# An S5 and mLSTM layer on one core: an early load moved to another buffer, a banked output projection, and eight weight scales computed earlier

## Chip, core and metric

The kernel runs on one core of a Trainium2 chip. The metric is the device time of one execution in microseconds (us). TensorE (PE) multiplies matrices into PSUM banks; VectorE (DVE) and ScalarE (ACT) read those banks; GpSimd (POOL) works on SBUF; all transfers are issued by SyncE (SP) on one queue, in order.

## What is computed

One layer on a sequence of 2048 positions with 1024 features: a norm, a projection that feeds two mixers side by side (an S5 state-space scan with a GLU, and four mLSTM heads), an output projection with residual, and a feed-forward network (FFN) with residual. Cut from the reference:

```
h = rmsnorm(x, norm_mix_g[l])
p = h @ w_in[l]
u, q_raw, k_raw, v, o_raw, i_raw, f_raw = jnp.split(p, cuts, axis=-1)
y_ssm = s5_mixer(u, ...)
y_ml = mlstm_mixer(q_raw, k_raw, v, o_raw, i_raw, f_raw, ...)
x = x + jnp.concatenate([y_ssm, y_ml], axis=-1) @ w_out[l]
h = rmsnorm(x, norm_ffn_g[l])
x = x + jnp.square(jax.nn.relu(h @ w_ff1[l])) @ w_ff2[l]
return rmsnorm(x, final_norm_g)
```

## The kernel before

Every product of large matrices is made from three matmuls of 16-bit halves (hi*hi, hi*lo, lo*hi), so every weight block is loaded as 32-bit numbers into a staging buffer, its largest absolute value is found, a power of two is derived from it as scale, and the block is split into two 16-bit halves.

For the weights of the projections, load_w does this: it loads into `st`, a tile of the pool stg, which has one buffer, so a load waits until the block before it has been split. w_scale (L107 to L122) reduces the tile on VectorE (mx, m), spreads the maximum over all partitions with one matmul against the identity (pmx, all_max, L98), reduces that (ma, L100) and derives the scale sg. L140, L141 and, for the u block, L134 to L137 split. The names end in vo0, qk0 and u0 for the first blocks that are used.

At the start the sequence is read in 16 tiles xt0 to xt15 of 128 positions (norm_x: L438 to L441 norm them into xs, L446 transposes xs on TensorE into pt, L448 and L449 split pt into xn). Products of the first half with vo0 (pv), qk0 (pq) and u0 (pu) follow. The S5 tiles uz0 and uz1, in the pool big, receive pu.

After sixteen mLSTM blocks and the S5 units the output projection runs: out_proj(t, m) makes one 128x512 tile, for a quarter t of the sequence and a tile m of eight features, from 24 matmuls into a PSUM tile po (mm3, L159 to L161). VectorE then adds it to x (L1053, the only reader of po, which so frees its bank), and squares are summed for the next norm (L1027, L1028). t=0 is mixed with the GLU of the S5 branch, t=1 runs alone, t=2 and t=3 alternate together with hprep, which prepares the seven operands of the FFN (one level of Strassen-Winograd; L1087 to L1123). The column sums ss_f and the rows rb_f are the FFN's norm. w_out comes in four blocks st_out0 to st_out3 through load_w; the residual tiles come as x2_0 to x2_3 (accx) and, for t of 2 and 3, tile by tile.

The FFN runs over 16 units of w1 (a0 to a15) and of w2 (b0 to b15), in two phases. In phase 0 every unit's scale is made when it has been loaded: f_scale (L1201 reduces 128x2048 to one column, pmx_a or pmx_b spreads it, six small operations follow), called by w1_scale and w2_scale. w_split (L1231, L1232) splits. fx, fv and fw are the products with w1, read into e and split into hid; gx, gv and gw those with w2, added to x by L1452.

PSUM has eight banks: pools psm (3, tag mm: pv, pq, pu, and glu's pgl), psl (3, tag ml: transposes, pmx, ss, rb) and psa (2, tag ax: po among others). The order of instructions on each engine is set by a scheduler when the program is built, by its own simulated times; the source order is its input. Tiles of one tag share buffers in turn.

Of the kernel before, what the change touches and what calls it, by code (L numbers as in the profile page):

```python
# [47 lines left out]
def trunk(  # L48
# [75 lines left out]
            V.tensor_scalar(out=sg[:, 0:1], in0=rs, scalar1=16384.0, scalar2=None, op0=ALU.mult)  # L124
        return sg, mp

    def load_w(src, K, N, ga, name, slot=0, wp=None, tag=None, E=V):
        st = stg.tile([P, K, N], F32, name=f"st_{name}", tag="stg")
        nc.sync.dma_start(out=st, in_=src)
        wt = (wp or wpool).tile([P, 2, K, N], F16, name=f"w_{name}", tag=tag or f"w{slot}")  # L130
        sg, mp = w_scale(st, K, N, ga, name)
        if ga is not None and E is G:
            for k in range(K):
                V.tensor_scalar(out=st[:, k, :], in0=st[:, k, :], scalar1=sg[:, k:k + 1], scalar2=None, op0=ALU.mult)  # L134
                if k % 2 == 1:
                    S.activation(out=wt[:, 0, k - 1:k + 1], in_=st[:, k - 1:k + 1], func=AF.Copy)
                    G.tensor_tensor(out=wt[:, 1, k - 1:k + 1], in0=st[:, k - 1:k + 1], in1=wt[:, 0, k - 1:k + 1], op=ALU.subtract)  # L137
        elif ga is not None:
            for k in range(K):
                S.activation(out=wt[:, 0, k, :], in_=st[:, k, :], func=AF.Copy, scale=sg[:, k:k + 1])  # L140
                V.scalar_tensor_tensor(out=wt[:, 1, k, :], in0=st[:, k, :], scalar=sg[:, k:k + 1], in1=wt[:, 0, k, :], op0=ALU.mult, op1=ALU.subtract)  # L141
        else:
            fl = st.rearrange("p k n -> p (k n)")
            hi = wt[:, 0].rearrange("p k n -> p (k n)")
            lo = wt[:, 1].rearrange("p k n -> p (k n)")
            S.activation(out=hi, in_=fl, func=AF.Copy, scale=sg[:, 0:1])
            V.scalar_tensor_tensor(out=lo, in0=fl, scalar=sg[:, 0:1], in1=hi, op0=ALU.mult, op1=ALU.subtract)
        return wt, mp
# [49 lines left out]
    mpa = r_ctx.enter_context(pool("mlsa", side="right"))  # L198
    l_ctx = ExitStack()
    big = l_ctx.enter_context(pool("big"))  # L200
    uz = [big.tile([P, NG, P], F32, name=f"uz{h}", tag="uz", bufs=2) for h in range(2)]
    gcon = l_ctx.enter_context(pool("gcon"))
    zmx = gcon.tile([P, 2, 4], F32, name="zmx")
    xr_dram = xT.rearrange("(k p) t -> p k t", p=P)
# [216 lines left out]
    with pool("start", side="right") as sp:  # L421
# [55 lines left out]
        load_vo(0)  # L477
        for b in range(4):
            load_x(b)
        norm_x(0)  # L480
        norm_x(1)
        proj_vo(0, 0)
        load_qk(0)
        norm_x(2)
        norm_x(3)
        proj_vo(0, 1)
# [7 lines left out]
        for j in range(8):  # L494
            u_proj(0, 0, (j,))
            xdone = norm_x(8 + j)
        gates_out(0)
        u_proj(1, 0)
        gates_out(1)
        load_u(1)  # L500
# [495 lines left out]
    x2f = drp.tile([P, KD, 2 * TB], F32, name="x2f")  # L996
    hopd = [drp.tile([P, 2, 4, TB], F16, name=f"hopd{i}") for i in range(7)]

    for mp in range(4):
        accx[mp] = accxp.tile([P, 2, 2, TB], F32, name=f"x2_{mp}", tag=f"ax{mp}")  # L1000
        nc.sync.dma_start(out=accx[mp].rearrange("p m c t -> p m (c t)"), in_=xr_dram[:, 2 * mp:2 * mp + 2, 0:2 * TB])

# [27 lines left out]
    def out_proj(t, m):  # L1030
# [5 lines left out]
        else:  # L1036
# [2 lines left out]
            else:  # L1039
                dst = xo[:, (2 * m + t - 6) % 8, :]  # L1040
            nc.sync.dma_start(out=dst, in_=xr_dram[:, m, t * TB:(t + 1) * TB])
        po = psa.tile([P, TB], F32, name=f"po{t}{m}", tag="ax")
        wt = wo[m // 2]
        mo = slice((m % 2) * P, (m % 2) * P + P)
        pairs = []
# [165 lines left out]
    def w1_load(ph, u, wp=None, tag=None):  # L1211
        raw = raw1[ph, u] = (wp or wpool).tile([P, 4, 512], F32, name=f"r1_{ph}{u}", tag=tag or f"w{u % 2}")
        nc.sync.dma_start(out=raw, in_=w1[u])

    def w1_scale(ph, u):
        raw = raw1[ph, u]
        if ph == 0:
            mp1[u], sg1[u] = f_scale(raw.rearrange("p s n -> p (s n)"), f"a{u}")
            if u % 2 == 1:

                mg = sc1(f"mg{u}")
# [42 lines left out]
    def w2_scale(ph, v):  # L1264
        raw = raw2[ph, v]
        if ph == 0:
            mp, sg2[v] = f_scale(raw.rearrange("p m s n -> p (m s n)"), f"b{v}")
            dd = dd2[v] = sc1(f"dd{v}")
            mg = mp1["g", v // 2]
            V.tensor_scalar(out=dd, in0=mg, scalar1=mg, scalar2=Mg2, op0=ALU.mult, op1=ALU.mult)  # L1270
            V.tensor_scalar(out=dd, in0=dd, scalar1=mp, scalar2=None, op0=ALU.mult)
# [25 lines left out]
        nc.sync.dma_start(out=mlr[t], in_=ml_d[t])  # L1297

    load_ml(0)
    load_ml(1)  # L1300
    load_wo(3, wp=r3, tag="wo3")
    glu_step(9)
    for n in range(10, NGL):
        out_proj(0, n - 10)
        glu_step(n)
    glu_c(NGL - 2)
# [14 lines left out]
    for m in range(KD):  # L1321
        out_proj(1, m)
        if m == 0:
            w1_load(0, 0, stg, "stg")
        if m == 1:
            rb0[0] = rms_rows(psum_colsum([accs[0]], TB, psl, "ml", "f0"), 4, ones_h, psl, "ml", "f0")
        if m == 3:
            w1_scale(0, 0)
        if m in (4, 5, 6):
            w1_prep(0, 0, m - 4)  # L1330
    for m in range(KD):
        out_proj(2, m)
        if m == 0:
# [2 lines left out]
            hprep(0, (None, 0, 1, None, 2, 3)[m], rb0)  # L1336
        if m == 4:
            w1_load(0, 1)
        if m == 7:
            w1_scale(0, 1)  # L1340
        out_proj(3, m)
    l_ctx.close()
# [320 lines left out]
```

## Time and profile before

| | before |
|---|---|
| median of 3 runs | 2167.97 us (2165.42 to 2172.41) |
| the profiled execution, its own time | 2163.71 us |
| its span from first to last instruction | 2161.7 us |
| TensorE clock granted, mean of full speed | 0.982 |

Where the time goes in the span: to 62 us the start, to 180 the u products and the gates, to 690 the mLSTM blocks and S5 units, to 925 the GLU's end and the output projection, to 1440 the FFN's phase 0, to 2110 phase 1, then the end. Durations below come from the profiled execution. A matmul's listed duration contains its passage through the array and overlaps its neighbour's, so the pace of a product is read from the distance of its neighbours.

### The profile page before, as it was taken

To read this page: it belongs to the slowest core of one execution; us is meant where nothing else is said; L and a number is where in the kernel's file an instruction comes from. 1 tells how busy PE (TensorE), PEld (TensorE's weight loads), DVE (VectorE), ACT (ScalarE), POOL (GpSimd) and SP (SyncE) were. 2 spreads that over 40 slices of the span, in tenths; PEclk is the share of its full clock that TensorE was granted. 3 is DMA by queue.
4 is the path that set the end of the run, shared out by engine and by line. 5 is a ranking of instruction groups with operands and counts; after the bars stand their busy time and mean duration, and the time that the engine had idled before them with its cause. 6 is when DMAs were issued, how large, how long until landed. Compare 5 with 4: busy or idle time off the path is not lost.

```text
span 2161.7 us, 30038 instructions
## 1 busy us (share of the span) xinstructions
PE 2030.1 (94%) x11205; PEld 1157.4 (54%) x11205; DVE 1694.4 (78%) x2850; ACT 1090.4 (50%) x2078; POOL 1082.9 (50%) x988
## 2 busy tenths in 40 slices
PE   6999898998999799999999999999999999999996
PEld 4987676766677444444444444444444444444445
DVE  7878888886857745769898898988787787777776
ACT  5436556555545423255454554555555555455543
POOL 2124546453210102365666766675685667665645
PEclk9999999999999999999999999999999999999998
DMA  4211211212103312311222222225332322121112
GB/s 168 70 52 50 60 40 45 64 41 58 59 20 107 118 40 88 102 49 51 86 88 69 97 74 78 83 79 195 136 137 87 109 98 93 44 78 40 39 40 79
DMA packets 55731, 168.18 MB, mean 78 GB/s; under 512 B 7904, under 2 KB 21408, under 8 KB 43040
## 3 DMA queue, kind: packets, MB, share of 16 engines
q1 hardware_dynamic: 55584, 166.26, 23.1%
q8 instruction: 88, 1.44, 0.3%
q14 instruction: 59, 0.48, 0.1%
HBM read 129.44 MB, written 28.41 MB: 73 GB/s over the span
## 4 chain that ended last, share of the span: by engine, by line
PE 52%; DVE 28%; POOL 6%; DMA 5%; ACT 4%; issue 4%; SPq 1%; POOLq 0%; DVEq 0%; ACTq 0%
DVE w2o L1232 3%; DMA r<-in_w_dram 3%; PE gx L1356 3%; PE gx L1358 3%; PE gx L1357 3%; PE fx L1357 3%; PE fx L1356 3%; PE fx L1358 3%; DVE x L1452 3%; PE po L159 2%; PE po L161 2%; PE po L160 2%; DVE y L247 2%; PE gv L1358 1%; PE gv L1356 1%
## 5 line engine op out<-in xcount | busy, mean ns | idle before, releaser
L1231 ACT ACTIVATE w2o<-r,fs_b 128x768 f16<-128x768 f32 (+1 forms) x128 | 105.2, 824 | 148.5 <-POOL r L1289 70.5
L1232 DVE SCALAR_TENSOR_TENSOR w2o<-r,fs_b,w2o 128x768 f16<-128x768 f32 (+1 forms) x128 | 138.6, 1084 | 29.7 <-ACT w2o L1231 29.3
L1357 PEld LDWEIGHTS <-w2o 128*128 128x128 f16 x952 | 93.3, 98 | 127.1 <-issue 31.1
L1385 ACT ACTIVATE e<-e 128x512 f32<-128x512 f32 x96 | 60.2, 628 | 196.9 <-DVE e L1421 95.6
L1356 PEld LDWEIGHTS <-w2o 128*128 128x128 f16 x952 | 93.5, 98 | 103.3 <-ACT w2o L1231 2.5
L1358 PEld LDWEIGHTS <-w2o 128*128 128x128 f16 x952 | 93.3, 98 | 103.6 <-DVE w2o L1232 2.7
L159 PE MATMUL pv<-w_vo,xn 128*128 128x256 f16 x512 | 140.8, 275 | 0.9 <-ACT xn L448 0.9
L161 PE MATMUL pv<-w_vo,xn 128*128 128x256 f16 x512 | 140.9, 275 | 0.4 <-DVE xn L449 0.3
L160 PE MATMUL pv<-w_vo,xn 128*128 128x256 f16 x512 | 140.7, 275 | 0.0
L1452 DVE SCALAR_TENSOR_TENSOR x2b<-gx,dd,x2b 128x512 f32<-128x512 f32 x112 | 82.8, 744 | 42.5 <-PE gx L1358 42.1
L1289 POOL TENSOR_TENSOR r<-r,s 128x256 f32<-128x256 f32 x64 | 65.1, 1018 | 101.6 <-DVE w2o L1232 101.6
L1245 POOL TENSOR_TENSOR s<-r 128x512 f32<-128x512 f32 x32 | 52.5, 1642 | 106.5 <-issue 72.9
L1452 DVE SCALAR_TENSOR_TENSOR x<-gx,dd,x 128x512 f32<-128x512 f32 x128 | 94.3, 741 | 6.6 <-PE gx L1358 6.5
L1356 PE MATMUL fx<-hop,wB 128*128 128x512 f16 x256 | 97.0, 379 | 0.9 <-ACT e L1414 0.9
L159 PE MATMUL pq<-xn,w_qk 128*128 128x512 f16 x256 | 97.5, 382 | 0.0
L160 PE MATMUL pq<-xn,w_qk 128*128 128x512 f16 x256 | 97.5, 381 | 0.0
L161 PE MATMUL pq<-xn,w_qk 128*128 128x512 f16 x256 | 97.5, 381 | 0.0
L1358 PE MATMUL fx<-hop,wB 128*128 128x512 f16 x256 | 97.0, 379 | 0.0
L1357 PE MATMUL fx<-hop,wB 128*128 128x512 f16 x256 | 97.0, 379 | 0.0
L159 PEld LDWEIGHTS <-xn 128*128 128x128 f16 x768 | 87.8, 114 | 10.9 <-ACT xn L448 1.6
L160 PEld LDWEIGHTS <-xn 128*128 128x128 f16 x768 | 87.6, 114 | 9.1 <-issue 0.4
L161 PEld LDWEIGHTS <-xn 128*128 128x128 f16 x768 | 87.5, 114 | 9.0 <-DVE xn L449 1.8
(1326 smaller groups left out, 6890.1 us busy)
## 6 DMA issues: line engine op xcount, KB each, us to landing
r<-in_w_dram SPq DMA_DIRECT2D x64, 1024.0 KB, 4.9
xt<-in_xN_dram SPq DMA_DIRECT2D x16, 512.0 KB, 4.5
rt<-rh SPq DMA_DIRECT2D x64, 128.0 KB, 2.3
hopd<-ho SPq DMA_DIRECT2D x28, 256.0 KB, 2.5
hop<-hopd SPq DMA_DIRECT2D x7, 1024.0 KB, 4.8
st_vo<-in_wvo_dram SPq DMA_DIRECT2D x4, 1024.0 KB, 5.1
st_qk<-in_wqk_dram SPq DMA_DIRECT2D x4, 1024.0 KB, 5.0
bcm<-negM_d SPq DMA_DIRECT2D x16, 256.0 KB, 3.2
```

The source lines that it names most:

```text
L159: T.matmul(out, wh, xh, start=(i == 0), stop=False)
L160: T.matmul(out, wh, xl, start=False, stop=False)
L161: T.matmul(out, wl, xh, start=False, stop=(i == n - 1))
L1231: S.activation(out=hi, in_=src, func=AF.Copy, scale=sg)
L1232: V.scalar_tensor_tensor(out=lo, in0=src, scalar=sg, in1=hi, op0=ALU.mult, op1=ALU.subtract)
L1245: G.tensor_tensor(out=s12[:, 0], in0=raw[:, 2], in1=raw[:, 3], op=ALU.add)
L1289: G.tensor_tensor(out=r[:, 1], in0=r[:, 1], in1=s12[:, 1], op=ALU.subtract)
L1356: T.matmul(out, wh, xh, start=(first and i == 0), stop=False, skip_group_check=True)
L1357: T.matmul(out, wh, xl, start=False, stop=False, skip_group_check=True)
L1358: T.matmul(out, wl, xh, start=False, stop=(last and i == n - 1), skip_group_check=True)
L1385: S.activation(out=x, in_=x if src is None else src, func=AF.Relu, scale=scale)
L1452: V.scalar_tensor_tensor(out=acc[:, j, c, :], in0=bk[b], scalar=dd, in1=acc[:, j, c, :], op0=ALU.mult, op1=ALU.add)
```

## The change

1. The first qk block is loaded into a tile st_q of the pool big, in the buffer that uz1 takes later, right after the first four x tiles are requested; load_w takes it as given.
2. The four residual tiles accx are requested one by one between the GLU steps, and so is the second of the mLSTM tiles (load_ml).
3. For t>0 and odd m, po is a tile of psm instead of psa.
4. scan_load loads four weight units into buffers of hop (the FFN operands, not yet in use), scan reduces each of them and makes the four scales in one set of small operations. It is called twice in the projection of t=1, for a2, a3, b0, b1 and for a4, a5, b2, b3. w1_scale and w2_scale take these scales instead of calling f_scale. The units are loaded again when they are used. w1_scale(0, 1) moves from m=7 to m=6.

```diff
-    def load_w(src, K, N, ga, name, slot=0, wp=None, tag=None, E=V):
-        st = stg.tile([P, K, N], F32, name=f"st_{name}", tag="stg")
-        nc.sync.dma_start(out=st, in_=src)
+    def load_w(src, K, N, ga, name, slot=0, wp=None, tag=None, E=V, st=None):
+        if st is None:
+            st = stg.tile([P, K, N], F32, name=f"st_{name}", tag="stg")
+            nc.sync.dma_start(out=st, in_=src)
...
+        st_q = big.tile([P, KD, 256], F32, name="st_q", tag="uz", bufs=2)
+        nc.sync.dma_start(out=st_q, in_=wqk[0])
         norm_x(0)
         norm_x(1)
         proj_vo(0, 0)
-        load_qk(0)
+        load_qk(0, st_q)
...
-    for mp in range(4):
+    def load_acc(mp):
         accx[mp] = accxp.tile([P, 2, 2, TB], F32, name=f"x2_{mp}", tag=f"ax{mp}")
...
-        po = psa.tile([P, TB], F32, name=f"po{t}{m}", tag="ax")
+        po = psm.tile([P, TB], F32, name=f"po{t}{m}", tag="mm") if t > 0 and m % 2 else psa.tile([P, TB], F32, name=f"po{t}{m}", tag="ax")
...
+    def scan_load(blocks, ids):
+        ts = []
+        for (kind, i), hi_ in zip(blocks, ids):
+            t_ = hopb.tile([P, 2048], F32, name=f"sc_{kind}{i}", tag=f"hop{hi_}")
+            nc.sync.dma_start(out=t_, in_=w1[i].rearrange("p s n -> p (s n)") if kind == "a" else w2[i].rearrange("p m s n -> p (m s n)"))
+            ts.append(t_)
+        return blocks, ts
+
+    def scan(bt):
+
+        blocks, ts = bt
+        n = len(blocks)
+        nm = "".join(f"{k}{i}" for k, i in blocks)
+        m1, ma, mp, sg = (scal.tile([P, n], F32, name=f"{v}_{nm}") for v in ("s1", "sa", "sm", "sg"))
+        for i, t_ in enumerate(ts):
+            V.tensor_reduce(out=m1[:, i:i + 1], in_=t_, axis=AX.X, op=ALU.max, apply_absolute_value=True)
+        pm = psl.tile([P, n, P], F32, name=f"pms_{nm}", tag="ml")
+        for i in range(n):
+            T.matmul(pm[:, i, :], m1[:, i:i + 1].to_broadcast([P, P]), ident, start=True, stop=True)
+        V.tensor_reduce(out=ma, in_=pm, axis=AX.X, op=ALU.max)
...
+        for i, b in enumerate(blocks):
+            scanned[b] = mp[:, i:i + 1], sg[:, i:i + 1]
...
-            mp1[u], sg1[u] = f_scale(raw.rearrange("p s n -> p (s n)"), f"a{u}")
+            mp1[u], sg1[u] = scanned.get(("a", u)) or f_scale(raw.rearrange("p s n -> p (s n)"), f"a{u}")
...
     load_ml(0)
-    load_ml(1)
+    load_acc(0)
     load_wo(3, wp=r3, tag="wo3")
     glu_step(9)
     for n in range(10, NGL):
+        if n in (10, 12, 14):
+            load_acc((n - 8) // 2)
+        if n == 13:
+            load_ml(1)
...
             w1_load(0, 0, stg, "stg")
+            sc_ = scan_load([("a", 2), ("a", 3), ("b", 0), ("b", 1)], (2, 3, 4, 5))
...
             w1_scale(0, 0)
+            scan(sc_)
+            sc_ = scan_load([("a", 4), ("a", 5), ("b", 2), ("b", 3)], (6, 2, 3, 4))
...
+        if m == 7:
+            scan(sc_)
```

What this does to the order, at three places. First the queue of SP at the start; xt are x tiles, A a small table, st_qk0, st_q and st_u0 weight blocks. Before:

```order
L430 DMA xt3_202<-in_xN_dram 128x1024
L316 DMA A_1281<-in_s5a_dram 128x96
L430 DMA xt4_430<-in_xN_dram 128x1024
L430 DMA xt5_489<-in_xN_dram 128x1024
L129 DMA st_qk0_298<-in_wqk_dram 128x2048
L430 DMA xt6_549<-in_xN_dram 128x1024
L430 DMA xt7_609<-in_xN_dram 128x1024
L430 DMA xt8_658<-in_xN_dram 128x1024
L129 DMA st_u0_452<-in_wu0_dram 128x2112
```

After:

```order
L431 DMA xt3_201<-in_xN_dram 128x1024
L482 DMA st_q_203<-in_wqk_dram 128x2048
L317 DMA A_1281<-in_s5a_dram 128x96
L431 DMA xt4_429<-in_xN_dram 128x1024
L431 DMA xt5_488<-in_xN_dram 128x1024
L130 DMA st_u0_451<-in_wu0_dram 128x2112
L431 DMA xt6_548<-in_xN_dram 128x1024
```

The qk block stands ahead of xt4 and xt5, and the u block ahead of xt6 instead of behind xt8. On VectorE the qk block's reduction now stands between the sixth and the seventh of the eight operations that split w_vo0, and the u block's in front of ma_qk0; on TensorE the matmul pmx_u0 stands 25 pq matmuls earlier.

Second, VectorE in the projection of t=1; x are residual tiles, po products, acc sums of squares, s_a2a3b0b1 and s_a4a5b2b3 (cut short) the columns of maxima. Before:

```order
L1053 SCALAR_TENSOR_TENSOR x_0_8193<-po_8782,ds_out_7480,x_0_8193 128x512
L1053 SCALAR_TENSOR_TENSOR x_0_8193<-po_8811,ds_out_7480,x_0_8193 128x512
L1060 TENSOR_SCALAR v_f_8845<-ss_f_8840 128x4
L1028 TENSOR_TENSOR acc_8781<-acc_8781,sq_w_8837 128x512
L1064 TENSOR_TENSOR dg_f_8848<-ident,v_f_8845 128x512
L1053 SCALAR_TENSOR_TENSOR x_1_8195<-po_8852,ds_out_7859,x_1_8195 128x512
L1028 TENSOR_TENSOR acc_8781<-acc_8781,sq_w_8878 128x512
L1053 SCALAR_TENSOR_TENSOR x_1_8195<-po_8881,ds_out_7859,x_1_8195 128x512
L100 TENSOR_REDUCE ma_a_8914<-pmx_a_8912 128x1
```

After:

```order
L1236 TENSOR_REDUCE s_a2a3b0b_8930<-sc_a_8811 128x1
L1057 SCALAR_TENSOR_TENSOR x_0_8210<-po_8782,ds_out_7480,x_0_8210 128x512
L1236 TENSOR_REDUCE s_a2a3b0b_8930<-sc_a_8813 128x1
L1057 SCALAR_TENSOR_TENSOR x_0_8210<-po_8819,ds_out_7480,x_0_8210 128x512
L1236 TENSOR_REDUCE s_a2a3b0b_8930<-sc_b_8815 128x1
L1064 TENSOR_SCALAR v_f_8853<-ss_f_8848 128x4
L1032 TENSOR_TENSOR acc_8781<-acc_8781,sq_w_8845 128x512
L1236 TENSOR_REDUCE s_a2a3b0b_8930<-sc_b_8817 128x1
L1068 TENSOR_TENSOR dg_f_8856<-ident,v_f_8853 128x512
L1057 SCALAR_TENSOR_TENSOR x_1_8289<-po_8860,ds_out_7859,x_1_8289 128x512
L1236 TENSOR_REDUCE s_a4a5b2b_9086<-sc_a_8948 128x1
L1236 TENSOR_REDUCE s_a4a5b2b_9086<-sc_a_8950 128x1
```

Six of the eight new reductions stand between these evacuations (L1053, now L1057); the last two follow within nine rows.

Third, VectorE at the end of the projection; m_a and m_b are the maxima of units of w1 and w2. Before:

```order
L1053 SCALAR_TENSOR_TENSOR xo<-po_9529,ds_out_8161,xo 128x512
L1028 TENSOR_TENSOR acc_9095<-acc_9095,sq_w_9555 128x512
L1201 TENSOR_REDUCE m_a_9652<-r_01_9436 128x1
L1201 TENSOR_REDUCE m_a_9781<-r_02_9758 128x1
L1201 TENSOR_REDUCE m_b_9929<-r_00_9715 128x1
L1053 SCALAR_TENSOR_TENSOR xo<-po_9560,ds_out_8255,xo 128x512
L1053 SCALAR_TENSOR_TENSOR xo<-po_9591,ds_out_8255,xo 128x512
```

After:

```order
L1057 SCALAR_TENSOR_TENSOR xo<-po_9581,ds_out_8161,xo 128x512
L1032 TENSOR_TENSOR acc_9147<-acc_9147,sq_w_9607 128x512
L1205 TENSOR_REDUCE m_a_9642<-r_01_9488 128x1
L1057 SCALAR_TENSOR_TENSOR xo<-po_9612,ds_out_8247,xo 128x512
L1032 TENSOR_TENSOR acc_9104<-acc_9104,sq_w_9638 128x512
L1057 SCALAR_TENSOR_TENSOR xo<-po_9663,ds_out_8247,xo 128x512
```

The reductions of a2 and b0 are gone from this place.

## Rows read from the trace of the kernel before

**Rows 1.** The page's first part: busy us, share, instructions of each engine

```profile
PE 2030.1 (94%) x11205; PEld 1157.4 (54%) x11205; DVE 1694.4 (78%) x2850; ACT 1090.4 (50%) x2078; POOL 1082.9 (50%) x988
```

**Rows 2.** Windows: us, busy us (instructions) by engine, granted clock, DMA share, GB/s

```profile
60.00:180.00 120.00, 116.64 (x957) 106.22 (x956) 95.94 (x358) 48.30 (x109) 22.23 (x29) 0.99 0.19 58
...
920.00:1100.00 180.00, 171.54 (x802) 79.58 (x800) 149.26 (x213) 97.19 (x144) 115.60 (x95) 1.00 0.19 63
```

**Rows 3.** Timeline of TensorE at the start: start, us, instruction, [idle before it]

```profile
44.48 0.38 PE L98 MATMUL pmx_u<-ident,m_u 128*128 128x128 f32 x2
...
53.80 1.94 PE L446 MATMUL pt<-ident,xs 128*128 128x128 f32 x8 [6.42 <-DVE xs L441]
...
55.57 0.44 PE L159 MATMUL pu<-w_u,xn 128*128 128x264 f16 x1
```

**Rows 4.** Timeline of VectorE at the start

```profile
21.42 2.29 DVE L107 TENSOR_REDUCE mx_qk<-st_qk 128x8 f32<-128x2048 f32 x1 [1.28 <-DMA st_qk<-in_wqk_dram]
...
25.59 0.29 DVE L100 TENSOR_REDUCE ma_qk<-pmx_qk 128x1 f32<-128x128 f32 x1 [0.95 <-PE pmx_qk L98]
...
39.04 2.35 DVE L107 TENSOR_REDUCE mx_u<-st_u 128x8 f32<-128x2112 f32 x1 [0.92 <-DMA st_u<-in_wu_dram]
```

**Rows 5.** TensorE in the output projection: waits from 840 to 925, then timeline

```profile
PE po L159 <- DVE xo L1053: 7.1, 4, 3.3
...
860.65 0.59 PE L159 MATMUL po<-ms,w_out 128*128 128x512 f16 x1 [3.29 <-DVE xo L1053]
...
913.42 0.38 PE L159 MATMUL po<-ms,w_out 128*128 128x512 f16 x1 [2.17 <-DVE xo L1053]
```

**Rows 6.** Waits of TensorE from 925 to 1100: us, times, longest

```profile
PE gx L1356 <- DVE x L1452: 4.8, 4, 2.8
...
PE pmx_a L98 <- DVE e L1405: 2.1, 2, 1.2
```

**Rows 7.** Waits of TensorE in the whole span

```profile
PE pmx_out L98 <- DVE m_out L110: 8.5, 1, 8.5
```

**Rows 8.** Timeline of the DMA queue: time of issue

```profile
1.74 2.30 SPq L430 DMA_DIRECT2D xt<-in_xN_dram  x4
...
16.64 0.33 SPq L129 DMA_DIRECT2D st_qk<-in_wqk_dram  x1
...
33.99 0.33 SPq L129 DMA_DIRECT2D st_u<-in_wu_dram  x1
...
711.96 0.33 SPq L129 DMA_DIRECT2D st_out<-in_wout_dram  x1
...
819.47 0.33 SPq L1262 DMA_DIRECT2D r<-in_w_dram  x1
```

**Rows 9.** DMA from 0 to 45 us, in 40 equal slices

```profile
GB/s 0 46 170 379 411 386 426 408 430 227 65 309 189 229 146 109 226 408 306 320 29 0 109 291 66 15 0 7 142 302 22 180 428 363 361 204 269 87 0 0
```

**Rows 10.** Timeline of VectorE in the projection of t=1

```profile
829.83 0.75 DVE L1053 SCALAR_TENSOR_TENSOR x<-po,ds_out,x 128x512 f32<-128x512 f32 x1 [2.98 <-PE po L161]
...
835.01 0.75 DVE L1053 SCALAR_TENSOR_TENSOR x<-po,ds_out,x 128x512 f32<-128x512 f32 x1 [2.98 <-PE po L161]
```

**Rows 11.** Windows in the output projection

```profile
780.00:838.00 58.00, 58.00 (x280) 27.80 (x279) 21.58 (x35) 11.89 (x17) 4.48 (x4) 1.00 0.18 60
...
860.00:880.00 20.00, 17.68 (x73) 7.52 (x73) 20.00 (x23) 8.90 (x15) 13.16 (x10) 0.91 0.24 78
...
892.00:906.00 14.00, 14.00 (x67) 6.37 (x65) 3.58 (x5) 1.89 (x3) 0.56 (x1) 1.00 0.41 131
```

**Rows 12.** Groups of VectorE from 900 to 1100: count, busy us, mean ns

```profile
L1201 DVE TENSOR_REDUCE m_a<-r 128x1 f32<-128x2048 f32 x7 | 15.9, 2278 | 4.0 <-DMA r<-in_w_dram 4.0
...
L1201 DVE TENSOR_REDUCE m_b<-r 128x1 f32<-128x2048 f32 x4 | 9.1, 2279 | 4.8 <-DMA r<-in_w_dram 4.8
```

**Rows 13.** Timeline of VectorE at the projection's end

```profile
906.04 4.48 DVE L1201 TENSOR_REDUCE m_a<-r 128x1 f32<-128x2048 f32 x2 [3.13 <-DMA r<-in_w_dram]
...
912.62 1.40 DVE L1053 SCALAR_TENSOR_TENSOR xo<-po,ds_out,xo 128x512 f32<-128x512 f32 x2
```

More of the change, by code (lines that the diff above doesn't have):

```diff
@@ L200, in trunk @@
     big = l_ctx.enter_context(pool("big"))
-    uz = [big.tile([P, NG, P], F32, name=f"uz{h}", tag="uz", bufs=2) for h in range(2)]
+    uz = [big.tile([P, NG, P], F32, name="uz0", tag="uz", bufs=2), None]
     gcon = l_ctx.enter_context(pool("gcon"))
@@ L210, in trunk, with load_qk @@
     SLOT_Q, SLOT_V = (0, 2, 1, 0), (1, 0, 2, 1)
-    def load_qk(h):
-        w, m = load_w(wqk[h], KD, 256, O_GMIX, f"qk{h}", SLOT_Q[h])
+    def load_qk(h, st=None):
+        w, m = load_w(wqk[h], KD, 256, O_GMIX, f"qk{h}", SLOT_Q[h], st=st)
         r_q = descale(m, 2.0 ** -25, f"q{h}")
@@ L497, in trunk @@
         gates_out(0)
+        uz[1] = big.tile([P, NG, P], F32, name="uz1", tag="uz", bufs=2)
         u_proj(1, 0)
@@ L1213, in w1_load @@
         nc.sync.dma_start(out=raw, in_=w1[u])
+    scanned = {}
+    def scan_load(blocks, ids):
[16 more added lines that the diff above has]
+        V.tensor_reduce(out=ma, in_=pm, axis=AX.X, op=ALU.max)
+        V.tensor_scalar(out=ma, in0=ma, scalar1=1e-30, scalar2=None, op0=ALU.max)
+        V.tensor_scalar(out=mp.bitcast(I32), in0=ma.bitcast(I32), scalar1=0x7F800000, scalar2=None, op0=ALU.bitwise_and)
+        V.reciprocal(sg, mp)
+        V.tensor_scalar(out=sg, in0=sg, scalar1=4096.0, scalar2=None, op0=ALU.mult)
+        for i, b in enumerate(blocks):
+            scanned[b] = mp[:, i:i + 1], sg[:, i:i + 1]
     def w1_scale(ph, u):
@@ L1266, in w2_scale @@
         if ph == 0:
-            mp, sg2[v] = f_scale(raw.rearrange("p m s n -> p (m s n)"), f"b{v}")
+            mp, sg2[v] = scanned.get(("b", v)) or f_scale(raw.rearrange("p m s n -> p (m s n)"), f"b{v}")
             dd = dd2[v] = sc1(f"dd{v}")
@@ L1338, in trunk @@
             w1_load(0, 1)
-        if m == 7:
+        if m == 6:
             w1_scale(0, 1)
```

## The prediction

> **What bounds the kernel now.** I read the engines' shares first: TensorE is busy 2030.1 us of the span, VectorE 1694.4 [rows 1]. A change that adds and removes no large matmul can therefore only win back TensorE's idle time, some 130 us. The windows say where that lies: almost none between 60 and 180 us, 8.5 us in 920 to 1100, where VectorE has 149.26 of 180 us to do [rows 2]. Then I read, for each of the four places that the change touches, what TensorE waits for.
>
> At the start TensorE sits idle for 6.42 us before the transposes of xs7, and its first u matmul starts at 55.57 [rows 3]. That chain begins with pmx_u0 at 44.48, which needs the maximum of st_u0, and VectorE begins that reduction, after waiting for the load, at 39.04 [rows 3, 4]. In the output projection four waits, together 7.1 us, the longest 3.29 and the last 2.17, all end when VectorE empties a product's bank [rows 5]. In the FFN TensorE waits 4.8 us for VectorE's L1452 and 2.1 us at pmx_a between 925 and 1100 [rows 6]. The fourth is the single wait of 8.5 us at pmx_out [rows 7].
>
> **Start: minus 4.9 us.** Before, st_qk0 is issued at 16.64, because it shares a buffer with st_vo0, and VectorE reduces it at 21.42 after waiting 1.28 us for it [rows 4, 8]. Now its load follows xt3 at about 4.1 us. By then st_vo0 and four x tiles, 3.1 MB, are asked for; at the 380 to 430 GB/s of the start [rows 9] they and the next 1 MB are in by about 13.2 (estimate). The reduction, 2.29 us, now stands inside w_vo0's split, so this split ends 2.3 us later, st_u0 is issued at about 18.9 instead of 33.99 [rows 8], and its maximum stands ahead of ma_qk0. There ma_qk0 waits for it: st_u0 is there some 5 us after its issue, and 2.3 us of reduction end at 26.2, against 25.59 for ma_qk0 before [rows 4]. That is a loss of 0.6 to 0.9 us. On TensorE pmx_u0 now stands ahead of 25 pq matmuls, which before ran ahead of it. One such matmul takes 0.216 us (24 of them per output product, whose evacuations are 5.18 us apart [rows 10]), so the chain can start 5.4 us earlier, and the 25 fill time that was idle. From 5.4 I take off 0.5 for the later ma_qk0, as TensorE has other products to run for part of that: 4.9. Bounds: 5.4 above; below a loss of 0.9, if the chain through xs7 does not shorten at all. TensorE has next to no idle time in the 120 us that follow [rows 2], so what is won stays won.
>
> **x tiles by pairs: 0.** The four x2 loads and the two hop loads stand in another order in front of the same st_out3 on the queue. What TensorE waits 8.5 us for [rows 7] is st_out3, issued at 711.96 [rows 8], when w_out2's split has freed its buffer; no load in front of it holds it. The order of TensorE's rows is unchanged there. I allow half a microsecond either way.
>
> **Banks for products: minus 7.9 us.** For t>0 every second product now takes one of psm's three banks, so five banks go round instead of two. TensorE may run four products ahead, 20.7 us, of an evacuation, and the longest wait was 3.29. The four waits go: 7.1 us. Behind the longest, which ends at 860.65, the granted clock of 860 to 880 is 0.91 [rows 11]: about 18% of it ran at 1.2 GHz instead of 2.4 after the engine had sat idle, which costs 1.8 us more. The row sums by themselves would give 6.1 without this clock and 7.9 with it; I take it in, since nothing else stops TensorE there. The Trainium skill (TensorE: Matmul & The Clock Gate, Part 1) says that an idle array falls back to half clock; by that the loss goes with its wait, and the trace agrees as far as one stretch at 0.91 can. Against this stands one new wait: the column sums of t=2 (ss_f2) share a bank with the last product po37 and wait for its evacuation, about 1.0 us (one L1053, 0.75 us [rows 10], and two handovers). Bounds: 8.9 without that wait, 1.2 if VectorE's own backlog holds TensorE in 850 to 892 all the same (rival 1).
>
> **Scan of eight weights: minus 4.5 us.** Added: eight loads of 1 MB (st_u0, of that size, took 5.05 us from issue to its reduction [rows 4, 8]) into hop buffers that lie empty, eight reductions of 2.28 us, eight small matmuls and two sets of small operations. Removed: the eight f_scale of a2 to a5 and b0 to b3, eight of the eleven L1201 there, thus 18.2 us of reductions and some 8 us of chains out of 906 to 1075 [rows 12]. The added reductions fall in 780 to 838, where VectorE has 21.58 of 58 us to do [rows 11]; 18.2 more leave it 18 us idle. There they delay evacuations by up to 4.6 us (two in a row), which the five banks cover; with two, a second bank covers 4.4 us (5.18 less 0.75 [rows 10]), and each further reduction in a row would cost TensorE its 2.2. They also push a0's preparation (L1232 after ma_a0) back by about 7 us, made up before 838, as hprep waits for rb_f1, not for it. The SP queue behind the loads: the later four wait until the first tiles are reduced, about 800; next behind them comes r2_00, before issued at 819.47 [rows 8], so there are some 15 us to spare. In the FFN the three reductions in front of two evacuations at 906.04 [rows 13] are down to one (its 2.17 us is counted above). Of the 8.5 us idle between 925 and 1100, the waits at pmx_a belong to a6 and a7, not scanned, and stay (2.1); the 4.8 at L1452 stem from a full VectorE, which now has some 26 of 149 us less. I take half of the idle time, 4.5. Bounds: 0 if these waits hang on the chain e to hid to gx and not on VectorE's load; 8.5 if all go.
>
> **Sum.** 4.9 + 0 + 7.9 + 4.5 = 17.3 us off. The profiled execution took 2163.7 us (its span is 2 us less), which gives 2146.4; the median of the three runs is 4.3 above that execution, so I predict 2150.7. Differences under 0.3%, 6.5 us, can't be told from no change.
>
> **Rivals.**
> 1. *VectorE, not the banks, bounds the projection.* In 860 to 880 it is busy 20.00 of 20 us [rows 11]. Then TensorE stalls with five banks as with two, and only the last wait goes, 2.17 less 1.0: in all 10.6 off, 2157.4. Against it: in 892 to 906 VectorE has just 3.58 of 14 us to do [rows 11], so its backlog can drain there while TensorE runs on. The Trainium skill (Perfetto Trace Analysis, Identifying the Most-Contended Engine) would optimize the engine with the highest occupancy first, here in this stretch VectorE; the trace bears that out for 20 us only.
> 2. *The start wins nothing* and loses 0.9, as ma_qk0 stands behind a load: 2156.5.
> 3. *Rivals 1 and 2 together*: 4.8 off, 2163.2, which counts as the same.
> 4. *All FFN waits go, and the start gives 5.4*: 21.8 off, 2146.2.
> 5. *Slower: the reductions stand one by one in TensorE's way.* In 785 to 817 VectorE works in order; a reduction that waits for its load or stands before an evacuation holds the bank behind it. If banks run out each time, the eight cost 18.2 us, and the projection gains nothing: 2163.7 + 18.2 - 4.9 - 4.5 = 2172.5, on the median 2176.8. It decides once VectorE's backlog passes four products, 20.7 us; with 36 us idle in 58 [rows 11] it should reach a quarter of that.
>
> **Chances and range.** My forecast 0.48, rival 1 0.15, rival 2 0.10, rival 3 0.11, rival 4 0.09, rival 5 0.07. Faster by over 0.3% hold the forecast and rivals 1, 2 and 4: 0.82. Within 0.3%: 0.11. Slower: 0.07. The forecast's own range, by its bounds of each term, is 2144 to 2158; the range that holds 8 in 10 takes in rivals 1, 2 and 4 with the spread of the runs: 2142 to 2162.
>
> **What would show it.** Start: st_q's reduction ends before 17, pmx_u0 near 39, the first u matmul near 50.8. Still 55 or more: rival 2. Pairs: the 8.5 us at pmx_out are still there. Banks: no wait of po for L1053 over 0.5 us in the projection, clock 1.00 throughout, the projection's last evacuation some 13 us earlier than before (4.9 and 7.9), and a wait near 1 us at ss_f2. Scan: eight reductions between 780 and 815 with TensorE at 20.00 of 20 us, VectorE some 26 us lighter in the 150 us after. The prediction is wrong if the waits for VectorE come back under another name: at rb_f1, at hprep's first operands, or at fx00.

## The result and the profile after

| | before | after |
|---|---|---|
| median | 2167.23 us (2165.42 to 2172.41, 4 runs) | 2149.57 us (2149.39 to 2150.49, 4 runs) |
| the profiled execution | 2163.71 us | 2149.39 us |
| mean granted clock in it | 0.982 | 0.979 |

The ratio is 0.9916, with a 95% interval of 0.9898 to 0.9933: 17.7 us faster, where 17.3 were forecast. The two profiled executions differ by 14.3 only.

First the engines' busy time in the page of the changed kernel, to be held against [rows 1]. TensorE does as much as before and VectorE almost as much; what went is idle time.

```profile
PE 2033.2 (95%) x11205; PEld 1160.0 (54%) x11205; DVE 1688.4 (79%) x2820; ACT 1090.1 (51%) x2078; POOL 1086.1 (51%) x988
```

The start, from the timelines of the DMA queue, VectorE and TensorE in the changed kernel, for [rows 3, 4, 8]:

```profile
4.13 0.49 SPq L482 DMA_DIRECT2D st_q<-in_wqk_dram  x1
...
18.51 0.33 SPq L130 DMA_DIRECT2D st_u<-in_wu_dram  x1
...
15.41 2.28 DVE L107 TENSOR_REDUCE mx_qk<-st_q 128x8 f32<-128x2048 f32 x1
17.61 0.87 DVE L142 SCALAR_TENSOR_TENSOR w_vo<-st_vo,sg_vo,w_vo 128x256 f16<-128x256 f32 x2
...
23.27 2.35 DVE L107 TENSOR_REDUCE mx_u<-st_u 128x8 f32<-128x2112 f32 x1 [0.88 <-DMA st_u<-in_wu_dram]
25.54 0.28 DVE L100 TENSOR_REDUCE ma_qk<-pmx_qk 128x1 f32<-128x128 f32 x1
...
38.58 0.39 PE L98 MATMUL pmx_u<-ident,m_u 128*128 128x128 f32 x2
...
48.71 1.16 PE L447 MATMUL pt<-ident,xs 128*128 128x128 f32 x8 [2.38 <-DVE xs L442]
50.03 0.33 PE L160 MATMUL pu<-w_u,xn 128*128 128x264 f16 x1 [0.15 <-ACT xn L449]
```

The reduction of st_q waits for nothing, st_u is issued 15.5 us earlier, and ma_qk does not start later than before (25.54 against 25.59). The wait for xs7 is down from 6.42 to 2.38, and the first u matmul starts 5.54 us earlier.

The waits of TensorE in the changed kernel from 640 to 785 (first row) and from 905 to 1300 (the others), for [rows 5 to 7]:

```profile
PE pmx_out L98 <- DVE m_out L110: 8.2, 1, 8.2
...
PE gx L1398 <- DVE x L1494: 9.0, 8, 3.6
PE gv L1398 <- DVE fm_b L1209: 1.7, 1, 1.7
...
PE ss_f L1078 <- DVE xo L1057: 0.8, 1, 0.8
```

The wait at pmx_out is as it was. From 780 to 925 no row has po any more; the column sums have the new wait.

The windows of the changed kernel (columns as in [rows 2]): t=1, t of 2 and 3, then the FFN up to the 721st fx (below).

```profile
785.00:840.00 55.00, 55.00 (x272) 27.28 (x271) 40.48 (x63) 10.88 (x15) 6.91 (x5) 1.00 0.50 194
840.00:912.00 72.00, 72.00 (x335) 32.77 (x333) 54.74 (x79) 25.22 (x41) 33.42 (x21) 1.00 0.29 99
914.12:1445.25 531.13, 513.78 (x2362) 233.99 (x2362) 445.90 (x587) 279.41 (x414) 362.32 (x300) 0.99 0.23 76
```

TensorE runs through both parts of the projection at full clock, 127 of 127 us. VectorE took the reductions in: part of its timeline there, and the small matmuls of the first set on TensorE.

```profile
793.55 2.28 DVE L1236 TENSOR_REDUCE s_a2a3b0b<-sc_b 128x1 f32<-128x2048 f32 x1
...
799.87 4.47 DVE L1236 TENSOR_REDUCE s_a4a5b2b<-sc_a 128x1 f32<-128x2048 f32 x2
804.91 0.75 DVE L1057 SCALAR_TENSOR_TENSOR x<-po,ds_out,x 128x512 f32<-128x512 f32 x1 [0.57 <-PE po L162]
...
804.93 1.06 PE L1239 MATMUL pms_a2a3b0b<-ident,s_a2a3b0b 128*128 128x128 f32 x8
```

To see where the time changes hands I take the start of the same matmul in each trace, and the distances between these starts. The marks are the first pu; the first, 193rd, 385th and last (768th) po, which stand at the beginning of t=0, t=1 and t=2 and at the end; then the first, 289th and 721st of the fx matmuls of the FFN, up to which the traces compared here hold the same products in somewhat different order; and the last gx.

| from mark to mark, us | before | after | difference |
|---|---|---|---|
| span's start to first pu | 55.57 | 50.03 | -5.54 |
| to first po | 666.94 | 668.50 | +1.56 |
| t=0 | 63.36 | 63.35 | 0.0 |
| t=1 | 43.76 | 45.55 | +1.79 |
| t of 2 and 3 | 93.93 | 84.55 | -9.38 |
| last po to first fx | 1.03 | 2.14 | +1.11 |
| fx 1 to 289 | 187.39 | 181.73 | -5.66 |
| fx 289 to 721 | 348.32 | 349.40 | +1.08 |
| to last gx | 681.50 | 681.52 | 0.0 |

These make 15.03; the end of the program is 1.0 us longer, which leaves the 14.0 us between the spans.

### The profile page after: what moved, and what is told of

It reads as the page before. It is cut to its first block, busy times and chain, and to the rows that moved or that the text cites. A ratio compares the mean times of both kernels' runs of the same rounds, so it can differ in the third digit from the quotient of the medians.

```text
span 2147.7 us, 30032 instructions
## 1 busy us (share of the span) xinstructions
PE 2033.2 (95%) x11205; PEld 1160.0 (54%) x11205; DVE 1688.4 (79%) x2820; ACT 1090.1 (51%) x2078; POOL 1086.1 (51%) x988
## 4 chain that ended last, share of the span: by engine, by line
PE 58%; DVE 23%; POOL 6%; DMA 5%; ACT 4%; issue 3%; SPq 1%; POOLq 0%; DVEq 0%; ACTq 0%
PE fx L1400 4%; PE fx L1398 3%; PE fx L1399 3%; PE gx L1398 3%; PE gx L1400 3%; PE gx L1399 3%; PE po L160 3%; PE po L162 3%; PE po L161 3%; DVE w2o L1265 2%; DMA r<-in_w_dram 2%; DVE x L1494 2%; PE fv L1400 2%; PE fv L1399 2%; PE fv L1398 2%
## 5 line engine op out<-in xcount | busy, mean ns | idle before, releaser
L162 PE MATMUL pv<-w_vo,xn 128*128 128x256 f16 x512 | 142.5, 278 | 2.5 <-DVE vx L440 2.5
L160 PE MATMUL pv<-w_vo,xn 128*128 128x256 f16 x512 | 142.3, 278 | 1.0 <-ACT xn L449 1.0
L161 PE MATMUL pv<-w_vo,xn 128*128 128x256 f16 x512 | 142.3, 278 | 0.0
L1264 ACT ACTIVATE w2o<-r,fs_b 128x512 f16<-128x512 f32 (+1 forms) x96 | 78.9, 824 | 113.8 <-POOL r L1322 52.6
L1265 DVE SCALAR_TENSOR_TENSOR w2o<-r,fs_b,w2o 128x512 f16<-128x512 f32 (+1 forms) x96 | 103.9, 1084 | 26.1 <-ACT w2o L1264 25.7
L1494 DVE SCALAR_TENSOR_TENSOR x2b<-gx,dd,x2b 128x512 f32<-128x512 f32 x112 | 82.8, 745 | 42.6 <-PE gx L1400 42.3
L1494 DVE SCALAR_TENSOR_TENSOR x<-gx,dd,x 128x512 f32<-128x512 f32 x128 | 94.4, 742 | 12.2 <-PE gx L1400 11.9
```

Of the source, the lines that this page charges most:

```text
L160: T.matmul(out, wh, xh, start=(i == 0), stop=False)
L161: T.matmul(out, wh, xl, start=False, stop=False)
L162: T.matmul(out, wl, xh, start=False, stop=(i == n - 1))
L1264: S.activation(out=hi, in_=src, func=AF.Copy, scale=sg)
L1265: V.scalar_tensor_tensor(out=lo, in0=src, scalar=sg, in1=hi, op0=ALU.mult, op1=ALU.subtract)
L1494: V.scalar_tensor_tensor(out=acc[:, j, c, :], in0=bk[b], scalar=dd, in1=acc[:, j, c, :], op0=ALU.mult, op1=ALU.add)
```

## The experiments

Each kernel but two is the changed one with the edit shown; ratios are to runs of the kernel before on the same chip (medians of 2166.87 to 2167.62).

**The first qk block staged as before.** The load goes back into stg; x pairs, banks and scan stay.

```diff
-        st_q = big.tile([P, KD, 256], F32, name="st_q", tag="uz", bufs=2)
-        nc.sync.dma_start(out=st_q, in_=wqk[0])
...
-        load_qk(0, st_q)
+        load_qk(0)
```

> The changed kernel, but with the first qk block staged behind vo0 as before. Theory (each part works where it stands, and the sum is additive): the first u matmul goes back from 50.0 to about 55.6 us in the trace; of these 5.5 us some 4 are still there at the start of the output projection, so 2153.6 to 2155.1 against 2149.6. Rival (the start wins nothing that lasts, because later loads set the time): 2149.6.

Measured: 2153.84 us, ratio 0.9942 (0.9929 to 0.9954), 4.3 above the changed kernel. Its timeline of TensorE has the old wait back:

```profile
54.91 1.94 PE L447 MATMUL pt<-ident,xs 128*128 128x128 f32 x8 [6.42 <-DVE xs L442]
56.69 0.44 PE L160 MATMUL pu<-w_u,xn 128*128 128x264 f16 x1
```

So this load alone shortens the start.

**Two banks.** All products back in psa.

```diff
-        po = psm.tile([P, TB], F32, name=f"po{t}{m}", tag="mm") if t > 0 and m % 2 else psa.tile([P, TB], F32, name=f"po{t}{m}", tag="ax")
+        po = psa.tile([P, TB], F32, name=f"po{t}{m}", tag="ax")
```

> The changed kernel with all products of the output projection in psa's two banks. Theory (banks were the limit): the waits of 7.1 us for evacuations and the lower clock behind the longest come back, 8.3 us at least, and the eight reductions of the scan, in a row of one or two in front of an evacuation, add up to 4 us more in t=1: 2158 to 2162. Rival (VectorE's own work bounds the projection, the banks are worth only the last wait): about 2150.8.

Measured: 2156.49 us, ratio 0.9944 (0.9931 to 0.9957), 6.9 above the changed kernel. Its waits from 780 to 925:

```profile
PE po L160 <- DVE xo L1057: 4.5, 2, 3.9
```

Both waits lie in t of 2 and 3, which take 92.30 us between the marks. In t=1, where the eight reductions stand, the marks are 45.54 apart, as with five banks: the reductions do not need the banks. The last wait of [rows 5], 2.17 us, stays away even with two banks, since only one unit is still reduced at that place. Banks and scan each remove it, and what they win does not simply add.

**No scan.** Both calls of scan_load and of scan are left out; every unit makes its scale by f_scale.

```diff
-            sc_ = scan_load([("a", 2), ("a", 3), ("b", 0), ("b", 1)], (2, 3, 4, 5))
...
-            scan(sc_)
-            sc_ = scan_load([("a", 4), ("a", 5), ("b", 2), ("b", 3)], (6, 2, 3, 4))
...
-            scan(sc_)
```

> The changed kernel without the scan: a2 to a5 and b0 to b3 get their scales in the FFN as before. Theory: the 4.6 us that the trace shows between the first and the last FFN unit are lost, the eight small matmuls (1.8 us in t=1) leave the projection, and the three reductions in front of the last evacuations are covered by five banks: about 2152.4. Rival A (the FFN's gain hangs on VectorE's order, not on the scan): 2149.6 or, without the small matmuls, 2147.8. Rival B (the reductions at the projection's end stall it in spite of five banks): 2154 or more.

Measured: 2153.70 us, ratio 0.9934 (0.9923 to 0.9946), 4.1 above. T=1 falls back to 43.76 and t of 2 and 3 stay at 84.55: five banks also cover the three reductions of [rows 13]. From the first to the 721st fx it takes 535.15 us, 4.02 more than the changed kernel. The scan thus costs 1.8 in t=1 and wins 4.0 in the FFN, 2.2 net; the rest of the 4.1 lies in stages that the edit does not touch.

The window between these marks, length first, then TensorE's busy time:

```profile
912.61:1447.76 535.15, 512.96 (x2378) 234.94 (x2378) 466.69 (x651) 280.09 (x416) 362.16 (x300) 1.00 0.22 76
```

TensorE is idle for 22.2 us of it, in the changed kernel for 17.4 of 531.13. This difference is steady from trace to trace. TensorE's order of products in the FFN is the same in the changed kernel, in the runs with qk as before, two banks, x tiles together and early st_out3, and with the scan alone: there it is idle for 16.7 to 17.5 us of this stretch. In the three kernels without the scan, again of one order, it is idle for 22.2 to 22.4. The length of the stretch is less steady, 527.0 to 531.1 with the scan (the changed kernel is at the upper end) and 535.2 to 535.7 without.

Among VectorE's own waits from 914 to 1060, and in the changed kernel no longer, are those of the reductions for their units:

```profile
DVE m_b L1205 <- DMA r<-in_w_dram: 4.3, 2, 3.4
...
DVE m_a L1205 <- DMA r<-in_w_dram: 1.1, 2, 0.7
```

**x tiles requested together.** The four residual tiles and the second mLSTM tile are requested together, as before.

```diff
+    for mp in range(4):
+        load_acc(mp)
...
-    load_acc(0)
+    load_ml(1)
...
-        if n in (10, 12, 14):
-            load_acc((n - 8) // 2)
-        if n == 13:
-            load_ml(1)
```

> The changed kernel with the four residual tiles and the second mLSTM tile requested at once, as before. Theory: nothing, 2149.6 within 0.5 us, and the wait at pmx_out stays near 8.2 us. Rival (the four loads in a row delayed what stood behind them): slower by the 1 to 2 us of the lost queue time, 2151.

Measured: 2149.50 us, ratio 0.9913 (0.9898 to 0.9927). This part does nothing.

**The fourth w_out block loaded early.** If the wait at pmx_out hangs on the load that must wait for stg, another buffer should end it. st_out3 goes into the buffer of the second mLSTM tile, behind the first one's load, and that tile is loaded after the GLU.

```diff
+    st_o3 = hopa.tile([P, KD, 256], F32, name="st_o3", tag="hop1")
+    nc.sync.dma_start(out=st_o3, in_=wout[3])
...
-    load_wo(3, wp=r3, tag="wo3")
+    load_wo(3, wp=r3, tag="wo3", st=st_o3)
...
-        if n == 13:
-            load_ml(1)
...
+    load_ml(1)
```

> The changed kernel, with the last block of w_out loaded into hop1's buffer, not yet in use, behind hop0ml; hop1ml follows when that block is split. Theory (the wait at pmx_out is the load queued behind w_out2's split, which the change in the order of the x tiles could not touch): the 8.2 us go, and part of the lower clock of 700 to 720 (0.66) with them: 2139 to 2142. Rival (the GLU chain behind pgT is not ready either): the wait moves to pgT or po, 2146 to 2148.

Measured: 2137.84 us (2135.17 to 2139.83), ratio 0.986 (0.9842 to 0.9877), 11.7 below the changed kernel. The windows of 690 to 785, the changed kernel first, then this one:

```profile
690.00:785.00 95.00, 80.48 (x397) 42.90 (x396) 61.52 (x139) 34.21 (x78) 9.65 (x13) 0.91 0.35 133
```

```profile
690.00:785.00 95.00, 87.72 (x443) 45.98 (x442) 68.69 (x143) 36.39 (x84) 10.63 (x13) 0.98 0.47 178
```

TensorE is busy 7.2 us more in that stretch, at a higher clock, and the row of pmx_out is gone from its waits. By the marks not all of the gain lies there: from the first pu to the first po this kernel takes 662.08 us, 6.4 less than the changed one; another 4.1 lie between the first and the 721st fx, where TensorE does the same products in the same order, and 1.4 in the end of the program. The two later kernels with the same early load take 658.90 and 658.25 us to the first po. So in its own place the load is worth 6.4 to 10.3 us.

**The eight reductions repeated in the FFN.** Scales come from the scan; each unit is reduced once more when it has come, into a column that nothing reads.

```diff
+            if ("a", u) in scanned:
+                V.tensor_reduce(out=sc1(f"mz{u}"), in_=raw.rearrange("p s n -> p (s n)"), axis=AX.X, op=ALU.max, apply_absolute_value=True)
...
+            if ("b", v) in scanned:
+                V.tensor_reduce(out=sc1(f"nz{v}"), in_=raw.rearrange("p m s n -> p (m s n)"), axis=AX.X, op=ALU.max, apply_absolute_value=True)
```

> The changed kernel with the scales from the scan, but with the eight reductions of a2 to a5 and b0 to b3 made a second time in the FFN, their results unused: VectorE's load is back there, the chain from reduction to scale is not. Theory (the FFN's 4.6 us were VectorE's load): 3 to 4.6 us lost, 2152.6 to 2154.2. Rival (they were the chain: waiting for the load, spreading matmul, small operations): at most 1 us lost, 2149.6 to 2150.6.

Measured: 2157.29 us, ratio 0.9946 (0.9932 to 0.996), 7.7 above, more than either theory. But the loss is not where the reductions are. From the first fx to the 289th this kernel takes 179.86 us, less than the changed one (181.73); it loses 9.8 from there to the 721st, behind the last added reduction, which ends by 1059. Its waits from 1100 to 1460 have a row

```profile
PE gx L1402 <- DVE x L1498: 14.2, 14, 2.6
```

where the changed kernel has 8.0 in 9. The added instructions also made the scheduler write another order of TensorE's FFN. TensorE is idle for 27.0 us from the first to the 721st fx, but only for 3.5 of them (3.6 in the changed kernel) up to the 289th, where six of the eight reductions stand. What part of the rest is VectorE's load and what part the other order, the run does not tell.

**Twelve weights scanned.** A third set, a6, a7, b4 and b5.

```diff
+            sd_ = scan_load([("a", 6), ("a", 7), ("b", 4), ("b", 5)], (5, 6, 2, 3))
...
-        if m == 7:
+        if m == 5:
             scan(sc_)
+        if m == 7:
+            scan(sd_)
```

> The changed kernel with a third set in the scan: a6, a7, b4 and b5. Theory (the same again, smaller): of TensorE's 13.7 us of waits between 914 and 1310 some 3 go, four small matmuls cost 0.9 in t=1, VectorE has the room: 2147 to 2148.5. Rival (VectorE is now full until hprep, evacuations and hprep come late): 2151 or more.

Measured: 2150.25 us, ratio 0.9918 (0.9904 to 0.9932): no gain. To the 289th fx it takes 181.49 us, 0.2 less than the changed kernel, and t=1 takes 0.7 more. The longest wait of the FFN's beginning, 3.6 us, is there still (3.5).

**The last two together.** Early st_out3 and twelve weights.

> The third set of the scan and the early load of the last w_out block together. Theory: the sum of the two, 2137 to 2141. Rival: what the one wins is given back at the other's place, not below 2144.

Measured: 2136.47 us (2136.27 to 2138.58), ratio 0.9855 (0.9842 to 0.9869), the best, and not to be told from the early st_out3 alone.

**Reductions scanned, chains kept.** The counterpart of the repeated reductions: the eight maxima come from the scan, but each unit spreads its own and makes its own scale in the FFN.

```diff
-    def f_scale(raw, nm):
+    def f_scale(raw, nm, m1=None):
...
-        m1 = smal.tile([P, 1], F32, name=f"m1_{nm}", tag="w_m1")
-        V.tensor_reduce(out=m1, in_=raw, axis=AX.X, op=ALU.max, apply_absolute_value=True)
+        if m1 is None:
+            m1 = smal.tile([P, 1], F32, name=f"m1_{nm}", tag="w_m1")
+            V.tensor_reduce(out=m1, in_=raw, axis=AX.X, op=ALU.max, apply_absolute_value=True)
...
-            mp1[u], sg1[u] = scanned.get(("a", u)) or f_scale(raw.rearrange("p s n -> p (s n)"), f"a{u}")
+            mp1[u], sg1[u] = f_scale(raw.rearrange("p s n -> p (s n)"), f"a{u}", scanned.get(("a", u)))
```

> The eight reductions stay in the projection of t=1, but each of the eight units makes its own scale in the FFN again: one small matmul (pmx) and some six small operations of VectorE, from the column that was scanned. Theory (the 2.28 us reductions on VectorE, and their waits for a unit's load, are what the scan takes away): 2149 to 2151, within 1.5 of the changed kernel; the eight small matmuls move from t=1 back into the FFN and cancel. Rival (the chain from maximum to scale is what TensorE waits for): the FFN loses what it lost without the scan, 2153 to 2155.

Measured: 2145.1 us (2143.27 to 2147.85), ratio 0.99 (0.9886 to 0.9914), below both theories. Its window between the marks:

```profile
911.75:1443.47 531.72, 513.57 (x2379) 235.57 (x2378) 459.20 (x645) 281.00 (x416) 363.28 (x300) 1.00 0.23 76
```

TensorE is idle for 18.2 us: of the 4.8 that the whole scan takes from the 22.2, the reductions make 4.0 and the chains 0.8. TensorE's order differs a little in this kernel too, so this split is an estimate. The small matmuls, 1.8, are back in the FFN and gone from t=1, and still the stretch takes only 0.6 more than in the changed kernel. What that loses again lies behind its longest wait. TensorE and VectorE in the changed kernel:

```profile
1069.35 0.58 PE L1398 MATMUL gx<-hd02T,w2o 128*128 128x512 f16 x1 [3.61 <-DVE x L1494]
```

```profile
1065.88 1.62 DVE L1105 TENSOR_TENSOR t2f<-b,t2f 128x512 f32<-128x512 f32 x1 [2.41 <-POOL hd04T L1091]
1067.43 1.20 DVE L1155 TENSOR_TENSOR b<-b,b 128x512 f32<-128x512 f32 x1
1068.56 0.74 DVE L1494 SCALAR_TENSOR_TENSOR x<-gx,dd,x 128x512 f32<-128x512 f32 x1
```

VectorE stood still for 2.41 us for GpSimd's hd04T, up to the moment at which TensorE's wait begins, and the evacuation that TensorE needs is queued two instructions behind. The clock follows:

```profile
1060.00:1070.00 10.00, 6.39 (x29) 2.76 (x28) 7.59 (x8) 3.26 (x5) 9.65 (x9) 0.91 0.39 131
1070.00:1080.00 10.00, 10.00 (x37) 4.22 (x36) 8.87 (x20) 3.45 (x6) 2.43 (x2) 0.75 0.00 1
```

With chains kept the longest wait is 1.6, and the clock of its window is 1.00. In t=1 and the FFN together this kernel is 1.2 us faster than the changed one. The rest of the 4.5 lies in stages that the edit does not touch.

**Banks alone, and scan alone, on the kernel before.** The kernel before with the edit of po, and the kernel before with the scan.

> The kernel before with the five banks and nothing else. By the stage account of the changed kernel (9.4 us won in t of 2 and 3, 1.1 given back at the column sums): 8.3 off the kernel before of this comparison, so about 2159.3. Rival (part of it was the scan's, whose reductions no longer stand at the projection's end): what taking the banks away cost, 6.9 or less, 2160.7 or more. Slower than 2163 would mean that the banks need the scan.

> The kernel before with the scan and nothing else, thus two banks under the added reductions. By the account: 4.6 won in the FFN, 2.2 at the projection's last wait, 1.8 paid for the small matmuls in t=1 and 0.4 for a stall there: about 4.6 off, so about 2163; by what is left of the whole change when the other two are taken out (17.7 less 6.9 less 4.3) 6.5 off, 2161. Rival (two banks cannot cover the reductions): 2166 or more.

Measured: 2156.79 us, ratio 0.9954 (0.9942 to 0.9967), and 2159.23 us, ratio 0.9965 (0.9952 to 0.9977); 10.1 and 7.6 faster, both more than expected. For the banks the difference is within the interval; for the scan the interval, 5.0 to 10.4 us, holds the 6.5 but not the 4.6 of the account. Their marks repeat the account: banks alone has 84.55 in t of 2 and 3 and 187.05 to the 289th fx, scan alone 92.38 and 181.84. The waits of scan alone from 780 to 925:

```profile
PE po L160 <- DVE xo L1057: 5.7, 3, 3.9
```

**Early st_out3 and kept chains together.**

> The run with the early load of the fourth w_out block and the run with each unit's own scale chain, put together. The first was 29.8 us below the kernel before of its comparison, the second 21.8, the changed kernel 17.7. If the two add, 33.9 below the kernel before of this comparison, about 2133. If what the kept chain won was chance of the clock but for the 1.8 us of small matmuls, 31.6 below, about 2135.3. If the kept chain loses in the FFN once that stage starts earlier, 2138 or more.

Measured: 2138.45 us, ratio 0.9868 (0.985 to 0.9885): the third case, and not to be told from the early st_out3 alone. It needs 530.85 us from the first to the 721st fx, the early st_out3 with scanned chains 527.03. That kernel too waits 3.3 us for VectorE at that place, but its clock stays at 1.00, so there is nothing to win by the shorter wait, and the eight small matmuls are paid in the FFN as they were in t=1. Of the 3.8 us they make 1.8 and TensorE's idle time 0.6 (17.20 against 16.65); the rest stays open.

## Why the prediction was right

The time (2150.7 against 2149.57) and the mechanisms of start and banks were right. The scan's term was too large: the clock behind a wait that stayed was put at nothing. The eight small matmuls were left out of the sum as well, but cancel. That the whole came so close is in part luck.

**Start.** 4.9 forecast, 5.54 to the first pu; undone, it costs 4.3. St_q's reduction ended at 17.69, not before 17, since it stands between two splits. pmx_u0 (38.58, forecast 39) and the first u matmul (50.03, forecast 50.8) came as said. The loss of 0.6 to 0.9 at ma_qk did not come. Rival 2 is out.

**x tiles by pairs.** 0 forecast, 0 measured; the 8.2 us at pmx_out stayed, and the early load shows that they were st_out3's, as the prediction read [rows 7, 8].

**Banks.** 7.9 net forecast, 9.38 less 1.11 = 8.3 found: the four waits (7.1) and 2.2 more, of which the clock of 0.91 in 860 to 880 explains the 1.8 forecast and the rest was not traced; against them the wait at ss_f2 (0.8 in its row, 1.1 between the marks; forecast 1.0). The last product starts 11.6 us earlier, not some 13: t=1 and the stretch before the first po took longer. Rival 1 is out: in a stretch where VectorE was full [rows 11], three more banks still gave TensorE all its waits back, and VectorE had room later (3.58 of 14 us busy in 892 to 906 before). Two banks in the changed kernel bring the waits back. The Trainium skill (Perfetto Trace Analysis, Identifying the Most-Contended Engine) would have started at VectorE, by its occupancy in this stretch; here buffers were enough.

**Scan in the projection.** That two banks would make each further reduction in a row cost 2.2 us was wrong: with two, t=1 took as long as with five; no more than two stand in a row there, 4.47 us together. Rival 5 is out with it. What the sum left out is TensorE's own work: the eight small matmuls cost t=1 1.79 us. They leave the FFN in exchange, so by themselves they win and lose nothing.

**Scan in the FFN.** 4.5 forecast, 4.57 found (5.66 less 1.08), but from other parts, and 2.8 net of what t=1 paid. Of the 8.46 us for which TensorE was idle up to the 289th fx, 3.61 are left, about half as forecast. But it is not the half that was meant: the waits at pmx_a (2.1), which were to stay, are gone, and of those for L1452 (now L1494) 3.6 us stayed in one piece, behind GpSimd, where less load on VectorE helps nothing. The longest wait before, and the stretch from the first to the 721st fx with its clock:

```profile
1056.43 0.38 PE L1356 MATMUL gx<-hd00T,w2o 128*128 128x512 f16 x1 [2.83 <-DVE x L1452]
```

```profile
924.59:1460.30 535.71, 513.27 (x2379) 234.94 (x2379) 467.58 (x652) 280.90 (x417) 363.05 (x300) 1.00 0.22 76
```

TensorE's idle time in this stretch fell by 5.1 (535.71 less 513.27 busy, 22.44, before; 17.35 after), the eight pmx left the stage (1.8, uncounted), and 2.3 went the other way. The clock is enough to explain them: it is 1.00 throughout before, and after the change 0.75 for the 10 us behind the wait of 3.61, so half of these ran at 1.2 GHz, which costs 2.5 us by the prediction's own reckoning for the banks (an estimate). This loss the sum had not counted.

The reason held in the main: with the reductions out and the chains kept, TensorE waits almost as little as with both out. But a full VectorE is only a part of it: a reduction also held VectorE until its unit had come. VectorE has 21.7 us less to do in the stretch (467.58 to 445.90), and the reductions of a2 and b0, 4.5 us, had stood in front of it: together the 26 forecast. Rival 4 had the start right (5.54), but is out, since 3.61 of the 8.46 us are left.

**Sum.** By the marks the start won 5.5, the banks 8.3 and the scan 2.8 net: 16.6, where 17.3 were forecast. Of these 1.6 were lost again between the first pu and the first po and 1.0 at the end, both in work that the change leaves alone, which makes the 14.0 between the spans. The prediction took its 17.3 off the median, which is sound: before's profiled run lay 3.5 below its later median of 2167.23, after's lies on its own. The medians differ by 17.7, with an interval of 14.5 to 22.1 that holds the 16.6. The terms were 0.6 and 0.4 too small for start and banks and 1.7 too large for the scan; that the median came within 1.1 us of the forecast is in part luck. The forecast's own range is no sum of its bounds either: added up, these give 2144.7 to 2168.2, not 2144 to 2158.

## What to carry to other kernels

Where an engine waits for evacuations in a stretch in which the evacuating engine is full, look whether that engine has room a little later; if so, more banks can cover the backlog, as they did here, and no work has to be moved. Where a computation is hoisted out of a busy stage, count its small matmuls at both places, ask which wait stays and what the clock does behind it, and read what is won from the idle time between two marks with the same work, since the scheduler writes another order around every edit. The longest single wait left was worth about as much as the best part of the change: one load into another buffer gave 11.7 us, 6.4 to 10.3 of them in its own place, where the banks alone had given 10.1.

## What the runs showed that was not expected

The same work takes several us more or less from run to run. From the last pu to the first po, where eleven of the fourteen kernels have the same order on TensorE and the mean granted clock is 0.95 or 0.96, the traces read from 559.64 to 563.71 us; a part worth 2 us can't be read off a span, only off marks around it.

A wait of about 3.5 us cost more than itself nearly every time. In front of the same gx matmul (of hd02T) TensorE waits for 3.29 to 3.69 us in eight of the kernels with the scan (all but the one that repeats the reductions and the two that keep the chains). In seven of them the granted clock of a 10 us stretch behind it fell to between 0.70 and 0.88, so part of it ran at 1.2 instead of 2.4 GHz. Only in the kernel with the early load, which has the shortest of these waits, no stretch there fell below 1.00:

```profile
1061.88 0.38 PE L1399 MATMUL gx<-hd02T,w2o 128*128 128x512 f16 x1 [3.29 <-DVE x L1495]
```

```profile
1060.00:1070.00 10.00, 8.04 (x38) 3.73 (x38) 9.90 (x19) 4.78 (x7) 4.62 (x4) 1.00 0.08 27
1070.00:1080.00 10.00, 10.00 (x48) 4.47 (x46) 7.89 (x13) 4.81 (x7) 5.61 (x4) 1.00 0.30 102
```

A shorter wait is no safe side: behind one of 2.14 us at 1382 the changed kernel has 0.83 in 1380 to 1390, and the kernel before, behind one of the same length at 1398, 1.00 in 1390 to 1410. The Trainium skill (TensorE: Matmul & The Clock Gate, A second HAM failure mode: psum-queue depth-cycling) describes a kernel in which frequent short idle times between groups of matmuls, as the PSUM banks are cycled, move the clock to and fro. No run here shows that: the loss here stands behind single waits.
